# A diffusion-transformer block on one core: weight combinations and weight norms made side by side in a room each, packed rotary tables, and attention's output weights split one stage earlier

## The chip, the core and the metric

The kernel runs on one core of a Trainium2 chip. The metric is device time in microseconds (us) from the program's start to its end. A core has five engines that take their instructions in order: TensorE (PE, matrix products; its weight loads are listed as PEld), VectorE (DVE), ScalarE (ACT), GpSimd (POOL) and SyncE (SP, which here only issues transfers, DMAs). Each engine waits on semaphores for what others produce, so an instruction that waits holds up everything behind it on its engine. The order of each engine's instructions is fixed when the program is built: a scheduler lays them out by a simulated timeline, and the kernel adds its own edges to it ("issue this after that").

## The reference, cut to what matters

One block over 2048 latent tokens of width 1024, with 256 context tokens (one batch, depth 1, float32):

```python
sh1, sc1, g1, sh2, sc2, g2 = split(silu(c) @ w_ada + b_ada)        # the same for the context's c_ctx
hx = rms_norm(x, norm1_g) * (1 + sc1) + sh1
fx, qx, kx, vx = split_projection(hx @ w_in)                        # 512 Fourier columns, 8 heads of 64
qx, kx = axial_rope(rms_norm(qx, q_norm_g)), axial_rope(rms_norm(kx, k_norm_g))
y_four = fourier_mix(fx)                                            # 2-D FFT, real part
y_attn = neighbourhood_attention(qx, kx, vx, kc, vc, rpb)           # 8 x 16 windows and all context keys
g_f, g_a = split(sigmoid(hx @ w_branch_gate))
mixed = (g_f * (y_four @ w_fourier_out) + g_a * (y_attn @ w_attn_out)) @ w_out
x = x + g1 * mixed
hx2 = rms_norm(x, norm2_g) * (1 + sc2) + sh2
x = x + g2 * (relu(hx2 @ w_mlp1) ** 2 @ w_mlp2)
```

## The kernel before

Every large product is made of float16 matmuls: each operand is split into a high and a low half by a scale that is a power of two, and three products of halves replace one product in float32. A scale needs a norm of its weights (a sum of squares over the whole matrix, or its largest row), so weights are read once for a norm and once for the split. The two MLP products use a scheme with 7 block products in place of 8, so their weights are read, combined by additions on DVE, split on ACT (high) and DVE (low), and written to DRAM as combinations ("blocks", `w1d` and `w2d`) that the MLP streams later.

**The projection stage** runs through eight pairs of 256-column units (`seq`): the Fourier columns; gates 4 and 5; query half 0 with gate 0; query half 1 with gate 1; values; key half 0 with gate 2; key half 1 with gate 3; gates 6 and 7. `run_pair(n)` runs pair n; the order of the matmuls is that of the program, and beside them side work is laid out by counting. After each tile of a unit comes `tick(share)`: a gate or Fourier tile counts 2, a 256-column tile of q, k or v counts 1. A tick advances two things. `pace[0]` steps per two ticks are taken of the generators in `beside` (first `side_work`). Once `side_work` has ended, the tick's share times a rate from `RATE[n]` is added to a counter, and each whole unit of it takes one step of `early_blocks`. A "step" is what a generator does up to its next `yield`. Everything in a tick is ordered behind the last eviction of a projection tile on ACT.

**What the side work is.** `side_work` sums the adaLN columns (`ada_load` fetches 1 MB, `ada_sum` makes two DVE sums of 128 x 1024), with the products of the rope tables and the q and k gains in between (`rope_products`), then takes the squares of the first four pieces of both MLP weights (`mlp_norms(range(4))`, a fetch of 1 MB into tile `w12m` and an ACT Square of 128 x 2048 each) and makes their scales (`mlp_scales(0)`). `early_blocks` then prepares six jobs of MLP blocks (`prepare`: each fetches 1 MB into `raw`, and makes 7 combinations; the fetch for the next job is issued in step 1 of the present one), the gate rows g1 and g2 (`gate_rows`), the squares of the other 24 pieces (`mlp_norms(range(4, 16))`) and their scales. All of these fetch into the two buffers of one tag, `awt`. `mlp_norms` holds two pieces: the Square of a piece comes after the fetch of the next but one. What is left of `early_blocks` when the last pair begins is issued there at once.

**The last pair** (gates 6 and 7) has `fourier_prep` beside it at a pace of four steps per tick: squares of the output weights (`norm`, one room `fn`), the folding of the Fourier columns, their channel transform (`channel_dft`, matmuls into `pc`), the split of the Fourier output weights, and small sums. Its last small step takes the norms of `w_attn_out` and `w_out` (`pwn`, a product with ones that sums over partitions) and makes `mgs[:, 0:1]`, the scale with which `w_attn_out` is split.

**Attention** then runs 64 places (4 pairs of heads x 4 row blocks x 4 column blocks) of two blocks each. `block` computes scores, bias and row maximum (one DVE instruction), the exponential (ACT), transposes (PE), the high half (ACT) and the low half (DVE) of the probabilities, and the product with the values. `step` interleaves the stages of consecutive blocks and takes `n_fill` steps of a filler, `beside_attention`: the merge of the Fourier branch (`merge_fourier`, 208 matmuls), then `load_wa`, which fetches `w_attn_out` on POOL's queue and splits it into tile `wa` in eight steps (one ACT and one DVE instruction of 128 x 512 each), and from place 54 on the first tile of the attention output (`attn_out(0)`). A second generator, `gating` (`output_weights`), fetches `w_out` and multiplies it by the gate row and splits it on POOL; `merge_fourier` takes two or three steps of it behind the stores of each of its eight parts. The filler gets one step per block, and from place 8 on a second one at every fourth block. At the last column block of a row block the attention output is transposed, scaled on ACT into `yo` and stored to `yA` from ACT's queue.

**The rope tables** (`load_rope`) hold the cosine and the sine twice, for q and for k: each of the four copies is fetched from a 2048 x 64 table into 128 partitions, so in pieces of 64 floats.

After attention come the output products (`po`) with the rest of the attention outputs, and the MLP with its block products (`pm`, `p`) in two halves of the tokens, beside which the other MLP blocks are prepared.

## Time and profile before

| | |
|---|---|
| median of 3 runs | 2572.53 us (2568.15 to 2574.7) |
| the profiled execution | 2573.11 us, span 2571.3 us |
| granted TensorE clock in it | 0.997 of full speed |
| busy | PE 2492.5 us, DVE 1774.4 us, ACT 1208.9 us, POOL 447.6 us |
| transfers | 509.50 MB, 198 GB/s on average |

The profiled execution's own time is 1.8 us more than its span. The profile gives, for each engine, when it was busy and, for an idle stretch, what ended it. A view by windows cuts the span into stretches and gives the busy time of each engine in them with the granted clock of TensorE (1.00 is full speed) and the busy share of the DMA engines; "x" numbers are counts of instructions. A view of one tile lists the instructions that write or read it, with the shortest, median and longest duration in ns. In a timeline a row ends in square brackets with the idle time before the instruction and what ended it. Matmuls are pipelined: one of 512 columns is listed with about 379 ns while the next starts after 216 ns, so busy time of PE is not a count of work, but idle time is time in which nothing ran. Line 85 (L85) is the matmul of a helper for all split products, and L1053 and L1054 are the two instructions of the helper `pair_of`; such groups are told apart by their tiles.

### The profile page before, as it was taken

The numbers are of one execution on the slowest core, as the hardware profiler recorded it, in microseconds if no ns is written. First come the engines' busy times: TensorE is split into PE (matmuls) and PEld (weight loads), VectorE is DVE, ScalarE is ACT, GpSimd is POOL, SyncE is SP. The second block draws the span as 40 slices with busy tenths as digits, with TensorE's granted clock in tenths as the row PEclk, the third lists the DMA queues.
The fourth block names the chain that finished last, engine by engine and source line by source line (L and its number), as shares of the span: only waits on it lengthen the run. The fifth ranks groups of instructions, "written<-read, shape, count | busy, mean of one in ns | idle before, by whom it ended". The sixth has DMA issues, their size and how long they took to land.

```text
span 2571.3 us, 41720 instructions
## 1 busy us (share of the span) xinstructions
PE 2492.5 (97%) x15706; PEld 1426.5 (55%) x15706; DVE 1774.4 (69%) x3592; ACT 1208.9 (47%) x2131; POOL 447.6 (17%) x567
## 2 busy tenths in 40 slices
PE   7999999999899999999999999999999999999999
PEld 4546668866554677786664444444444444444444
DVE  7755676574453888987885878979777635546367
ACT  7714544325553788964444646445450524223150
POOL 1101220021121567610000121211212000000000
PEclk9999999999999999999999999999999999999999
DMA  8784726547874576656778777777876433333334
GB/s 298 225 271 152 239 82 212 185 151 237 278 262 136 174 214 185 193 177 225 254 242 292 248 263 252 249 246 243 270 266 217 119 95 111 99 103 94 111 103 156
DMA packets 224866, 509.50 MB, mean 198 GB/s; under 512 B 33868, under 2 KB 87884, under 8 KB 209304
## 3 DMA queue, kind: packets, MB, share of 16 engines
q1 hardware_dynamic: 190632, 384.05, 46.6%
q0 software_dynamic: 27264, 91.59, 10.2%
q10 hardware_dynamic: 6768, 31.20, 3.6%
q8 instruction: 123, 2.02, 0.3%
q14 instruction: 79, 0.65, 0.1%
HBM read 367.26 MB, written 137.39 MB: 196 GB/s over the span
## 4 chain that ended last, share of the span: by engine, by line
PE 68%; DMA 11%; DVE 10%; ACT 5%; issue 4%; POOL 1%; SPq 0%; ACTq 0%; DVEq 0%; POOLq 0%
PE p L85 20%; PE pm L85 19%; PE po L85 5%; PE ps_g L85 4%; PE pua L85 2%; PE ps_f L85 2%; PE tp L1638 2%; PE ps_q L85 2%; PE ps_v L85 2%; DMA w12m<-in_w_mlp 2%; PE pv L1652 2%; PE pmf L1573 1%; DMA w12m<-in_w_mlp1t 1%; PE sc L1616 1%; DMA w1d<-wo 1%
## 5 line engine op out<-in xcount | busy, mean ns | idle before, releaser
L85 PE MATMUL pm<-hc,wb 128*128 128x512 f16 x2688 | 582.6, 379 | 5.6 <-DVE u L1935 3.5
L85 PE MATMUL p<-wb,a 128*128 128x512 f16 x2688 | 581.9, 379 | 2.3 <-DVE X L2060 1.7
L85 PEld LDWEIGHTS <-wb 128*128 128x128 f16 x2688 | 263.0, 98 | 323.5 <-issue 7.2
L85 PEld LDWEIGHTS <-a 128*128 128x128 f16 x2688 | 263.0, 98 | 320.0 <-issue 3.2
L2060 DVE SCALAR_TENSOR_TENSOR X<-p,msc,X 128x512 f32<-128x512 f32 x280 | 201.3, 745 | 157.3 <-PE p L85 139.0
L85 PEld LDWEIGHTS <-w_g 128*128 128x128 f16 x1536 | 150.3, 99 | 167.0 <-issue 0.9
L85 PE MATMUL ps_g<-hx,w_g 128*128 128x512 f16 x768 | 171.4, 379 | 0.0
L85 PE MATMUL ps_g<-hx_room,w_g 128*128 128x512 f16 x768 | 171.3, 379 | 0.0
L85 PE MATMUL po<-wo,mH 128*128 128x512 f16 x512 | 152.6, 379 | 1.3 <-DVE ga L1699 1.3
L1935 DVE TENSOR_TENSOR u<-pm,u 128x512 f32<-128x512 f32 x128 | 87.3, 688 | 84.4 <-PE pm L85 82.9
L414 ACT ACTIVATE wo<-ws,msc 128x512 f16<-128x512 f32 x96 | 69.0, 718 | 148.5 <-DVE ws L456 113.9
L1939 ACT ACTIVATE p<-pm 128x512 f32<-128x512 f32 x32 | 18.9, 590 | 239.3 <-PE pm L85 239.3
L1625 DVE CUSTOM_DVE_ANT_0 s<-sc,bt,qsc 128x736 f32<-128x736 f32 (+5 forms) x128 | 110.9, 866 | 21.3 <-PE sc L1619 15.0
L85 PEld LDWEIGHTS <-hx_room 128*128 128x128 f16 x1152 | 113.8, 99 | 19.0 <-DVE qn_k L608 1.6
L85 PEld LDWEIGHTS <-hx 128*128 128x128 f16 x1152 | 113.4, 99 | 18.0 <-DVE qn_k L608 1.9
L1646 DVE SCALAR_TENSOR_TENSOR pL<-tp,pH 128x640 f16<-128x640 f32 (+1 forms) x128 | 112.3, 877 | 11.1 <-ACT pH L1641 10.3
L2071 POOL DMA_DIRECT2D xr<-x1d x32 | 17.3, 540 | 569.3 <-DVE X L1935 563.1
L1629 ACT ACTIVATE s<-s,m 128x736 f32<-128x736 f32 (+5 forms) x128 | 104.7, 818 | 13.1 <-DVE m L1625 13.0
L414 ACT ACTIVATE wo<-raw,msc 128x512 f16<-128x512 f32 x128 | 87.9, 710 | 42.1 <-DVE raw L456 15.1
L1638 PE MATMUL tp<-ident,s 128*128 128x128 f32 x704 | 102.6, 280 | 4.5 <-ACT s L1629 4.3
L543 ACT ACTIVATE ot_g<-ps_g,usc_g 128x512 f32<-128x512 f32 x64 | 43.4, 681 | 132.7 <-PE ps_g L85 74.6
L415 DVE SCALAR_TENSOR_TENSOR wo<-raw,msc,wo 128x512 f16<-128x512 f32 x128 | 94.2, 744 | 15.1 <-ACT wo L414 15.0
(573 smaller groups left out, 4485.3 us busy)
## 6 DMA issues: line engine op xcount, KB each, us to landing
wb<-w1d SPq DMA_DIRECT2D x224, 256.0 KB
wb<-w2d SPq DMA_DIRECT2D x224, 256.0 KB
raw<-in_w_mlp ACTq DMA_DIRECT2D x24, 1024.0 KB
w2d<-wo POOLq DMA_DIRECT2D x86, 256.0 KB, 3.9
w1d<-wo POOLq DMA_DIRECT2D x84, 256.0 KB, 3.8
gT<-ot_g SPq DMA_DIRECT2D x64, 256.0 KB
w12m<-in_w_mlp1t SPq DMA_DIRECT2D x16, 1024.0 KB
w12m<-in_w_mlp SPq DMA_DIRECT2D x16, 1024.0 KB
```

What stands on the lines that cost most here:

```text
L85: last_mm[0] = pe.matmul(ps, l, r, start=(start and i == 0), stop=(stop and i == n - 1))
L414: act.activation(hi, src, AF.Copy, scale=scale)
L415: dve.scalar_tensor_tensor(out=lo, in0=src, scalar=scale, in1=hi, op0=ALU.mult, op1=ALU.subtract)
L543: last_out[0] = act.activation(o, ps, func, scale=scale, bias=bias)
L1573: pe.matmul(ps, l, r, start=(i == 0), stop=(i == len(prods) - 1))
L1625: tail["dve"] = dve.tensor_tensor_reduce(out=s[:, :n], in0=sc, in1=bias, op0=ALU.add, op1=ALU.min, scale=qsc[:, 4:5], scalar=3.0e38, accum ...
L1629: tail["act"] = act.activation(s[:, :n], s[:, :n], AF.Exp, bias=m1[:, 0:1], scale=-1.0, accum_out=m1[:, 1:2])
L1638: tail["pe"] = pe.transpose(tp[:, i * 128:(i + 1) * 128], s[:, o:o + 128], ident)
L1646: tail["dve"] = dve.scalar_tensor_tensor(out=pL[:, :c], in0=tp[:, :c], scalar=PTOP, in1=pH[:, :c], op0=ALU.mult, op1=ALU.subtract)
L1652: tail["pe"] = pe.matmul(pv, p_[:nk, i * 128:(i + 1) * 128], vv[:nk, h2 * 128 + o:h2 * 128 + o + 64], start=(j == 0 and i == 0), stop=(j = ...
L1935: last["dve"] = dve.tensor_tensor(out=o, in0=x, in1=y, op=op)
L2060: last["dve"] = dve.scalar_tensor_tensor(out=X[x], in0=ps, scalar=down if op == ALU.subtract else up, in1=X[x], op0=ALU.mult, op1=ALU.add)
```

## The change

- `ada_load`, `mlp_norms` and others take their room from `big_room`: two tags of one buffer, `awt0` and `awt1`, used in turn unless a number is given.
- `gate_rows` moves from behind the early MLP blocks to `side_work`, ahead of the first squares. The pace is 3 in pair 1 and 2 in pairs 2 to 6 (before: 3, 3, then 2).
- `early_blocks` keeps only the six jobs of blocks, all in room `awt0`; the fetch of the next job is issued in step 6, and each job ends in two empty steps. The other 24 squares become a generator of their own, `other_norms`, in room `awt1`: fetch, step, Square, step. Both run side by side with a rate each, in pairs 3 to 6.
- The rope tables are laid out on the host as 128 x 1024, fetched once each (into the half for q), and the products for k come before those for q.
- `w_attn_out` gets its norm, scale and split in `fourier_prep` (`attn_norm`, `attn_scale`, and twice `attn_load` and `attn_split`), with the halves stored to a DRAM scratch `waD`. In attention four fetches from `waD` on SP's queue replace `load_wa`; the filler's second step comes at every sixteenth block.
- `merge_fourier` takes `gating` steps after each half of a part, behind the copy that opens the part, one per half (two from part 4 on), and `output_weights` issues one fetch per step.
- `yA` is stored from SP's queue, and the low half of the first attention output tile (`yaL`) is made on DVE, not POOL.

The diff, cut to its core:

```diff
+    waD = scratch("waD", [4, 128, 2048], F16)
...
+    def big_room(name, i=None):
+        if i is None:
+            i = turn_of[0] = 1 - turn_of[0]
+        return pb.tile([128, KT, 256], F32, tag=f"awt{i}", name=name).rearrange("p k n -> p (k n)")
...
+        yield from gate_rows()
         yield from mlp_norms(range(N_OWN))
         yield from mlp_scales(0)
...
-                           2, sp.dma_start, sp.dma_start)
+                           2, sp.dma_start, sp.dma_start, False)
         del jobs[:N_EARLY]
-        yield from gate_rows()
-        yield from mlp_norms(range(N_OWN, 16))
+
+    def other_norms():
+
+        for kind in range(2):
+            for j in range(N_OWN, 16):
+                wt = big_room(f"w12m{kind}_{j}", 1)
+                sp.dma_start(wt, a[("w_mlp1t", "w_mlp2")[kind]][j])
+                yield
+                with tc.issue_after(last_out[0].ins):
+                    act.activation(wt, wt, AF.Square, accum_out=(w1m, w2m)[kind][:, j:j + 1])
+                yield
         yield from mlp_scales(1)
...
-                if j == 1:
+                if j == (1 if ahead else 6):
                     fetch(n + 1)
+                yield
+            if not ahead:
+                yield
                 yield
...
-    blocks = [early_blocks(), 0.0, False]
+    blocks, begun = [[early_blocks(), 0.0, 0.0], [other_norms(), 0.0, 0.0]], [False]
...
+            if begun[0]:
+                for o in blocks:
+                    o[1] += share * o[2]
+                    while o[1] >= 1.0:
+                        o[1] -= 1.0
+                        next(o[0], None)
...
             both = pb.tile([128, 2, 16, 64], F32, tag="r" + nm, name=f"r{nm}")
+            sp.dma_start(both[:, 0].rearrange("p t d -> p (t d)"), a[nm])
...
-    RATE = (0, 0, 0.2, 0.25, 0.5, 1.0, 0.9, 0)
+    RATE = ((0, 0),) * 3 + ((0.2, 0.3), (0.4, 0.45), (0.6, 0.55), (0.6, 0.55), (0, 0))
...
-        pace[0] = 8 if n == len(seq) - 1 else (0, 3, 3, 2)[min(n, 3)]
+        pace[0] = 8 if n == len(seq) - 1 else (0, 3, 2)[min(n, 2)]
...
+        def attn_norm():
+            dve.tensor_reduce(out=mgs[:, 12:13], in_=wn[:, 0:2], axis=AX.X, op=ALU.add)
+            spread(mgs[:, 7:8], mgs[:, 12:13], "pwa")
+            pool.tensor_tensor(mgs[:, 7:8], mgs[:, 7:8], half[:, 0:1], op=ALU.pow)
...
+        def attn_split(i):
+            for k in range(2):
+                o = (both[:, k] if i == 0 else (both[:, 1], mix[:, 1])[k]).bitcast(F16).rearrange("p (n o t) -> p n o t", n=2, o=2)
+                for n in range(2):
+                    pair_of(o[:, n, 0], o[:, n, 1], x_room[:, k, n * 512:(n + 1) * 512], mgs[:, 0:1])
+                    yield
+                sp.dma_start(waD[2 * i + k], o.rearrange("p n o t -> p (n o t)"))
...
+                with tc.issue_after(stored.ins):
+                    for _ in range(1 + (m >= 4)):
+                        next(gating, None)
             for h in range(2):
-                i = pool.dma_start(mF[m, :, h * 1024:(h + 1) * 1024], o[h])
-            with tc.issue_after(i.ins):
-                for _ in range(2 if m < 2 else 3):
-                    next(gating, None)
+                pool.dma_start(mF[m, :, h * 1024:(h + 1) * 1024], o[h])
...
-            act.dma_start(yA[hp, :, rb * 512:(rb + 1) * 512], yo)
+            sp.dma_start(yA[hp, :, rb * 512:(rb + 1) * 512], yo)
...
-        eng = dve if t else pool
+        eng = dve
...
-        yield from load_wa()
+        for k in range(4):
+            sp.dma_start(wa[:, k].rearrange("p n o t -> p (n o t)"), waD[k])
+        yield
...
-            step(block(hp, rb, cb, h2, yp), 1 + (n >= 8 and (2 * n + h2) % 4 == 0))
+            step(block(hp, rb, cb, h2, yp), 1 + (n >= 8 and (2 * n + h2) % 16 == 0))
```

More of the change, by code (lines that the diff above doesn't have):

```diff
@@ L341, in mlp_norms @@
             if kind < 2:
-                wt = pb.tile([128, KT, 256], F32, tag="awt", name=f"w12m{kind}_{j}", bufs=2).rearrange("p k n -> p (k n)")
+                wt = big_room(f"w12m{kind}_{j}")
                 sp.dma_start(wt, a[("w_mlp1t", "w_mlp2")[kind]][j])
@@ L477, in dit_block @@
     beside, pace = [side], [0]
-    ticks, rate = [0], [0.0]
-    blocks = [early_blocks(), 0.0, False]
+    ticks = [0]
+    blocks, begun = [[early_blocks(), 0.0, 0.0], [other_norms(), 0.0, 0.0]], [False]
     def tick(share):
@@ L490, in tick @@
                     if next(o, o) is o and o is side:
-                        blocks[2] = True
-            if blocks[2]:
-                blocks[1] += share * rate[0]
-                while blocks[1] >= 1.0:
-                    blocks[1] -= 1.0
-                    next(blocks[0], None)
+                        begun[0] = True
+            if begun[0]:
[4 more added lines that the diff above has]
+                        next(o[0], None)
     def load_raw(w, c0, name):
@@ L578, in load_rope @@
             both = pb.tile([128, 2, 16, 64], F32, tag="r" + nm, name=f"r{nm}")
+            sp.dma_start(both[:, 0].rearrange("p t d -> p (t d)"), a[nm])
             for i, qk in enumerate("qk"):
-                r = both[:, i]
-                sp.dma_start(r, a[nm].rearrange("(t p) d -> p t d", p=128))
-                rope[nm, qk] = r
+                rope[nm, qk] = both[:, i]
     def rope_products(i):
-        r, g = rope[("cos", "sin")[i // 2], "qk"[i % 2]], gain["qk"[i % 2]]
-        dve.tensor_tensor(out=r, in0=r, in1=g.unsqueeze(1).broadcast_to([128, 16, 64]), op=ALU.mult)
+        nm, qk = ("cos", "sin")[i // 2], "kq"[i % 2]
+        dve.tensor_tensor(out=rope[nm, qk], in0=rope[nm, "q"], in1=gain[qk].unsqueeze(1).broadcast_to([128, 16, 64]), op=ALU.mult)
     turned = []
@@ L710, in dit_block @@
     wide = [t.bitcast(F32).rearrange("p o k t -> p (o k t)") for t in hx_rooms]
-    x1_rooms = [pb.tile([128, KT, 256], F32, tag="awt", name=f"x1_{i}", bufs=2).rearrange("p k n -> p (k n)") for i in range(2)]
+    x1_rooms = [big_room(f"x1_{i}") for i in range(2)]
     ada_rooms = [wide[i][:, o:o + 2048] for i in (1, 0) for o in (0, 2048)]
@@ L894, in first_tokens @@
     def first_tokens():
-        r = [pb.tile([128, KT, 256], F32, tag="awt", name=f"h0{o}", bufs=2).bitcast(F16).rearrange("p k n -> p (k n)") for o in "HL"]
+        r = [big_room(f"h0{o}").bitcast(F16) for o in "HL"]
         r = [t.rearrange("p (k t) -> p k t", t=512) for t in r]
@@ L986, in run_pair @@
             return first_pair()
-        rate[0] = RATE[n]
-        pace[0] = 8 if n == len(seq) - 1 else (0, 3, 3, 2)[min(n, 3)]
+        for o, r in zip(blocks, RATE[n]):
+            o[2] = r
+        pace[0] = 8 if n == len(seq) - 1 else (0, 3, 2)[min(n, 2)]
         wu, new = pair(n), [load_pair_unit(n + 1, u) for u in range(2)] if n + 1 < len(seq) else []
@@ L1183, in fourier_prep @@
         yield
+        attn_norm()
         x_scale(1)
@@ L1187, in fourier_prep @@
         rows_split(1, 0)
+        attn_scale()
         yield
@@ L1214, in fourier_prep @@
         yield
+        yield from attn_split(0)
+        attn_load(1)
         x_square(3)
@@ L1223, in fourier_prep @@
         x_scale(3)
+        yield from attn_split(1)
         yield from channel_dft(3)
@@ L1267, in fourier_prep @@
         dve.tensor_reduce(out=mgs[:, 4:5], in_=g1r, axis=AX.X, op=ALU.max, apply_absolute_value=True)
-        for i, (j, n) in enumerate(((0, 2), (2, 4))):
-            dve.tensor_reduce(out=mgs[:, 12 + i:13 + i], in_=wn[:, j:j + n], axis=AX.X, op=ALU.add)
-        spread(mgs[:, 7:9], mgs[:, 12:14], "pwn")
-        pool.tensor_tensor(mgs[:, 7:9], mgs[:, 7:9], half[:, 0:2], op=ALU.pow)
+        dve.tensor_reduce(out=mgs[:, 13:14], in_=wn[:, 2:6], axis=AX.X, op=ALU.add)
+        spread(mgs[:, 8:9], mgs[:, 13:14], "pwn")
+        pool.tensor_tensor(mgs[:, 8:9], mgs[:, 8:9], half[:, 0:1], op=ALU.pow)
         yield
-        dve.tensor_copy(mgs[:, 6:7], mgs[:, 7:8])
-        power_of_two(mgs[:, 6:7], HTOP, 1.0e-9)
-        dve.reciprocal(mgs[:, 0:1], mgs[:, 6:7])
         o = mgs[:, 8:9]
@@ L1296, in dit_block @@
         if n == len(seq) - 1:
-            for o in beside + blocks[:1]:
+            for o in beside + [o[0] for o in blocks]:
                 for _ in o:
@@ L1703, in attn_out @@
             yield
-    def load_wa():
-        raws = [py.tile([128, D], F32, tag=f"y{k // 2}{'HL'[k % 2]}", name=f"wao{k}") for k in range(4)]
-        for k in range(4):
-            pool.dma_start(raws[k], a["w_attn_out"][0, k * 128:(k + 1) * 128, :])
-        for _ in range(6):
-            yield
-        for k in range(4):
-            for n_ in range(2):
-                pair_of(wa[:, k, n_, 0], wa[:, k, n_, 1], raws[k][:, n_ * 512:(n_ + 1) * 512], mgs[:, 0:1])
-                yield
     def beside_attention():
```

22 lines of the change are left out of this document (15 added, 7 removed).

## The prediction

> **What bounds the kernel now.** I read the page first, then the span cut into stretches along the projection pairs, then who waits for whom on PE and ACT, then the timeline at the longest PE wait, the chain of waits, and single tiles. The page's totals, then the stretches (pair 1 is 120 to 203, pairs 2 and 3 reach to 404, values to 500, the two key pairs to 600 and 706, last gates to 814, attention 840 to 1143, MLP from 1430):
>
> ```profile
> span 2571.3 us, 41720 instructions
> PE 2492.5 (97%) x15706; PEld 1426.5 (55%) x15706; DVE 1774.4 (69%) x3592; ACT 1208.9 (47%) x2131; POOL 447.6 (17%) x567
> ...
> core 0: us, PE busy (x) PEld busy (x) DVE busy (x) ACT busy (x) POOL busy (x), PEclk, DMA share, GB/s
> ...
> 120.00:203.00 83.00, 80.35 (x379) 36.86 (x377) 52.19 (x130) 22.83 (x28) 1.19 (x2) 1.00 0.73 239
> 203.00:288.00 85.00, 81.62 (x548) 54.30 (x547) 40.44 (x135) 38.25 (x69) 14.44 (x17) 0.98 0.61 209
> 288.00:404.00 116.00, 112.64 (x791) 77.78 (x789) 88.95 (x275) 57.65 (x121) 26.69 (x25) 1.00 0.44 150
> 404.00:500.00 96.00, 94.37 (x865) 84.27 (x864) 54.51 (x128) 36.17 (x67) 1.12 (x2) 1.00 0.50 166
> 500.00:600.00 100.00, 97.46 (x697) 68.33 (x695) 70.21 (x201) 33.19 (x63) 21.24 (x21) 1.00 0.50 161
> 600.00:706.00 106.00, 96.09 (x639) 64.28 (x638) 46.74 (x148) 63.65 (x93) 19.13 (x18) 0.97 0.85 289
> 706.00:814.00 108.00, 99.79 (x542) 53.86 (x541) 50.66 (x151) 48.60 (x76) 16.62 (x20) 1.00 0.54 190
> ...
> 840.00:1040.00 200.00, 193.15 (x2403) 151.43 (x2401) 172.71 (x399) 162.22 (x361) 128.27 (x126) 0.99 0.63 183
> 1040.00:1100.00 60.00, 53.87 (x754) 46.20 (x753) 56.25 (x124) 55.59 (x127) 37.47 (x35) 1.00 0.76 214
> 1100.00:1143.00 43.00, 41.30 (x565) 36.57 (x563) 39.10 (x90) 33.57 (x78) 8.18 (x8) 1.00 0.44 138
> ...
> 1430.00:2571.30 1141.30, 1130.04 (x5232) 511.62 (x5229) 789.15 (x1207) 430.03 (x687) 116.67 (x215) 1.00 0.55 178
> ```
>
> PE is the bound: 2492.5 of 2571.3 us. The change adds one tiny PE product and removes none, so it can gain only where PE idles: the stretch's length less PE's busy time. That is 9.9 us at 600 to 706, and there the clock column takes 3% of 106 = 3.2 us more: 13.1 us, the worst stretch. 203 to 404 has 3.4 + 3.4 idle and 2% of 85 = 1.7 in the clock: 8.5. 404 to 500 has 1.6, 500 to 600 has 2.5, the last gates 8.2, attention 6.9 + 6.1 + 1.7. The MLP's 11.3 are out of the change's reach.
>
> What makes the 13.1 us:
>
> ```profile
> ACT w12m L340 <- DMA w12m<-in_w_mlp: 19.3, 11, 3.1
> ACT w12m L340 <- DMA w12m<-in_w_mlp1t: 13.5, 8, 3.2
> ```
> ```profile
> L340 ACT ACTIVATE w12m<-w12m x32: 1901/1911/1916, 252.4 to 695.7; 128x2048 f32<-128x2048 f32 x32
> L340 ACT ACTIVATION_READ_ACCUMULATOR w12m<-w12m x32: 183/187/204, 254.2 to 697.5; 128x1 f32 x32
> ```
> ```profile
> 646.76 1.91 ACT L340 ACTIVATE w12m<-w12m 128x2048 f32<-128x2048 f32 x1 [3.05 <-DMA w12m<-in_w_mlp]
> 648.58 0.19 ACT L340 ACTIVATION_READ_ACCUMULATOR w12m<-w12m 128x1 f32 x1
> ...
> 648.93 0.37 ACT L644 ACTIVATE sH_k<-tq_k 128x256 f16<-128x256 f32 x1
> ...
> 649.40 0.41 DVE L645 TENSOR_TENSOR sL_k<-tq_k,sH_k 128x256 f16<-128x256 f32 x1
> ...
> 649.87 0.48 PE L634 MATMUL tq_k<-ident,qr_k 128*128 128x128 f32 x1 [4.36 <-DVE sL_k L645]
> ```
> ```profile
> 624.23 4.93 DMA w12m<-in_w_mlp1t
> ...
> 689.73 10.09 DMA fn<-in_w_fourier_out
> ```
>
> Twenty or so Squares come back to back. Each holds ACT for its wait on the fetch (32.8 us over 19 of them, 1.7 each) and then 1.91 + 0.19 us; behind it stand the key's evictions (sH_k), behind those DVE (sL_k), behind that PE, 4.36 us here. The chain of waits over this stretch is fetch, Square, fetch, Square; a fetch of 1 MB lands after 4.93 us at best there, and the slowest, a first one for the last gates, takes 10.09.
>
> **Norms and combinations side by side.** The same 24 fetches and Squares, and six jobs of combinations, are spread over pairs 4 to 6. Counting from the code: values give 36 shares, a key pair 34, so `other_norms` gets 16.2 + 18.7 + 18.7 of its 54 steps and one in pair 3; the combinations get 14.4 + 20.4 + 20.4 of their 56. Both end with the last key pair, and about one step is left to issue there. A share lasts 96 / 36 = 2.7 us in the values and 206 / 68 = 3.0 in the key pairs, so a Square comes every two steps, 11 to 12 us apart, where its single room needs 4.9 to 10.1 us for the fetch and 2.1 for the Square, 7 to 12 us. It fits, mostly. A Square that finds its fetch one step (5.5 us) old may hold ACT for 0 to 4.6 us, but then ACT has 6 us before the next, where now it has 2. Only six Squares are left in the last key pair. I expect it to idle like its sister pair now, 2.5 us with the same matmuls: 13.1 - 2.5 = **10 us gained**. The bounds are 13 (all of it) and -10 (the first rival below). Values and first key pair get eight or nine Squares each, and the first key pair loses the gate rows; I leave their 1.6 + 2.5 as they are. Combinations keep their instructions; their single raw room is refilled over three steps, 16 us, which covers 10.09.
>
> **Gate rows, pace.** They move from 500 to 535 into pairs 2 and 3:
>
> ```profile
> L281 DVE CUSTOM_DVE_ANT_0 awtg<-awtg,silb x16: 1215/1220/1226, 499.5 to 533.2; 128x1024 f32<-128x1024 f32 x16
> ```
> ```profile
> PE tq_k L634 <- DVE sL_k L645: 6.1, 2, 4.4
> PE pms L359 <- DVE msd L354: 3.6, 2, 3.4
> PE pu_g L520 <- DVE usc_g L521: 2.8, 1, 2.8
> ```
>
> 16 sums of 1.22 us are 19.5 us of DVE, and their 8 fetches queue on SP. DVE is idle 45 us in 203 to 288 and 27 in 288 to 404, and combinations leave pair 3. The `pms` wait (3.4 us, and the clock's 1.7 us right behind it) came of three steps between the last Square and PE's product at 1.5 steps a tick; at one a tick the product has half as much time again. Against that, gate rows, Squares and scales fill 203 to 404 to the last tick but two. I take 3 of its 8.5 us as gained (0 to 6).
>
> **Last gates.** They get 8 more steps of 51 (64 are offered): 8 halves on ACT and on DVE, two 1 MB fetches and four stores on SP in front of the norm fetches and the gate stores, and a sum over partitions (`pwa`) one step behind a Square:
>
> ```profile
> L1053 ACT ACTIVATE wa<-wao,mgs x8: 736/760/775, 1056.2 to 1068.2; 128x512 f16<-128x512 f32 x8
> L1054 DVE SCALAR_TENSOR_TENSOR wa<-wao,mgs,wa x8: 725/736/2496, 1057.8 to 1070.1; 128x512 f16<-128x512 f32 x8
> ```
> ```profile
> 812.93 0.16 DVE L1079 COPY mgs<-pwn 128x2 f32<-128x2 f32 x1 [16.30 <-PE pwn L1078]
> ```
>
> That is 6 us on each of two engines that are idle half of these 108 us. PE idles 8.2 us for 51 steps, so 1.3 us for 8 more, and 0.7 for `pwa`: **2 us lost**. If all eight pairs and both fetches stood on the path it would be 8 x (0.76 + 0.74) + 5 = 17. The cover is DVE's 16.3 us of idleness before the last step; gone, the last small sums slip into the sequence transform behind it, which doesn't read them.
>
> **Attention.** The eight splits leave 1056 to 1073, where DVE is the bound (56.25 of 60 us) and PE idles 6.1. DVE loses 7 x 0.74 + 2.5 = 7.6 us, and the merge, at 17/16 steps a block for 5/4, reaches from place 43 to 49, so that this idle stretch has matmuls. I take the whole 6.1. Added is the low half on DVE, at the stretch where it is busy 39.10 of 43:
>
> ```profile
> L1682 DVE TENSOR_TENSOR yaL<-yat,yaH x7: 1206/1215/1226, 1125.5 to 1321.3; 128x1024 f16<-128x1024 f32 x7
> L1682 POOL TENSOR_TENSOR yaL<-yat,yaH x1: 2137/2137/2137, 1095.4 to 1095.4; 128x1024 f16<-128x1024 f32 x1
> ```
> ```profile
> L1666 ACTq DMA_DIRECT2D yA<-yo x16: 326/326/350, 869.7 to 1144.6; - x16
> ```
>
> 1.2 us on DVE, so **5 us gained** (-4 to 9). The 16 stores free 5.2 us of ACT, which isn't the bound: nothing. On SP they stand among prefetches whose buffers come free no earlier than the row block that the store ends. The `wa` fetches wait on SP for the last merge matmul at place 49; queued behind them is the next q. Eight blocks later, about 15 us, PE needs them: 2 MB behind one another, about 10 us at twice 4.93. If they came late, PE would lose up to 4. `gating` keeps its work, and each piece moves ahead of the `mF` stores on POOL, which is idle 72 of 200 us: nothing, down to 2 us lost where a bias table queues behind it.
>
> **Rope tables.** Two fetches for four, of 4 KB pieces for 256-byte ones.
>
> ```profile
> L581 SPq DMA_DIRECT2D rcos<-in_cos x2: 647/3567/6487, 72.4 to 73.1; - x2
> L586 DVE TENSOR_TENSOR rcos<-rcos,gaink x1: 1218/1218/1218, 131.5 to 131.5; 128x1024 f32<-128x1024 f32 x1
> ```
>
> They are issued near 72 and first read at 131, and PE idles 2.7 us in all of 120 to 203: nothing. The Trainium skill ("DMA: Bandwidth & Descriptors", Specifications) asks for transfers of at least 512 bytes for line rate; by it the queue would empty sooner; no row here shows the two sizes apart, and it moves no term of this sum.
>
> **Sum.** -10 - 3 + 2 - 5 = -16 us from 2573.1 (the profiled execution, 0.6 above the median): **2557 us**. Bounds of the terms together reach 2545 to 2565.
>
> **The rivals.**
> (1) The single room holds ACT, slower. If a fetch lands later than about 9 us, the room's cycle passes 11 us and every Square meets an unlanded fetch, now through all of 404 to 706. At the present price, 13.1 us per 106, that is 302 / 106 x 13.1 = 37 us in place of 17.2: +20, and +14 with the other terms: 2587. For: one fetch of 10.09, and combinations now fetch and store beside. Against: the rows near 5 us were taken at a DMA share of 0.85, which spreading lowers. The Trainium skill ("Trainium Kernel Development and Optimization", Best Practices) asks for two buffers so that transfers overlap compute; by that rule this is the likely case, but the trace's waits are from two rooms. Chance 0.09.
> (2) The waits move with the Squares: 24 of them cost 13.1 wherever they stand. Then -3 + 2 - 5: 2567. Chance 0.13.
> (3) The last gates run over by the 17 us above: 2572. Chance 0.07.
> (4) A generator falls behind, its Squares come at once where the last gates begin, at 4 us each for three: 2569. The count speaks against it. Chance 0.04.
> The forecast keeps 0.67. A measurement here tells about 0.3%, 7.7 us, from no change. Faster by more (below 2565): the forecast, and some of (2): 0.70. Slower by more: (1), and a bad end of (3): 0.11. The rest 0.19. The range leaves out (1) and the far tail below: 2543 to 2573.
>
> **What would show it.** Right: PE idle near 3 us and clock 1.00 in the last key pair; Squares about 11 us apart with waits below 4; no `wa` splits after 1040 and PE idle under 2 there; the last gates' idle near 10. Wrong: more than 60 us of ACT waiting on `w12m`, a PE wait over 3 us on tq_k with the clock below 1.00 behind it, or PE waiting on `wa` or on `pc` for a split.

## The result: 22 us faster, more than forecast, and partly in other places

The changed kernel takes 2548.5 us (median of 5 runs, 2540.68 to 2548.97), the kernel before beside it 2570.19 us (5 runs, 2568.15 to 2574.7). The ratio is 0.9904, 95% interval 0.989 to 0.9919. The profiled execution is the one of 2548.5 us; its span is 24.6 us shorter than that of before (2571.3 - 2546.7). The forecast was 16 us.

The page's totals of the changed kernel first:

```profile
span 2546.7 us, 41747 instructions
PE 2490.3 (98%) x15708; PEld 1428.7 (56%) x15708; DVE 1774.9 (70%) x3594; ACT 1210.8 (48%) x2131; POOL 444.0 (17%) x563
```

PE's busy time, in which slowed matmuls count too, is 2.2 us less than before (2492.5), so 22.4 of the 24.6 us are idle time of PE. Where they went is read from the first and last starts of the same tiles. The view of single tiles, kernel before (the last two times in a row are the group's first and last start):

```profile
L85 PE MATMUL ps_q<-w_q,hx x384: 269/273/417, 212.9 to 392.7; 128*128 128x256 f16 x192
...
L85 PE MATMUL ps_v<-w_v,hx x384: 269/273/273, 398.2 to 495.5; 128*128 128x256 f16 x192
...
L85 PE MATMUL ps_k<-w_k,hx x384: 269/273/283, 495.6 to 693.3; 128*128 128x256 f16 x192
...
L1619 PE MATMUL sc<-k,Q x256: 271/272/417, 840.1 to 1136.2; 128*128 128x256 f16 x128
...
L85 PE MATMUL po<-wo,mH x512: 376/379/379, 1151.6 to 1393.5; 128*128 128x512 f16 x171
```

The same rows of the changed kernel:

```profile
L85 PE MATMUL ps_q<-w_q,hx x384: 269/273/421, 211.7 to 393.5; 128*128 128x256 f16 x192
...
L85 PE MATMUL ps_v<-w_v,hx x384: 269/273/273, 399.0 to 494.1; 128*128 128x256 f16 x192
...
L85 PE MATMUL ps_k<-w_k,hx x384: 269/273/283, 494.2 to 674.2; 128*128 128x256 f16 x192
...
L1663 PE MATMUL sc<-k,Q x256: 271/272/421, 814.9 to 1112.9; 128*128 128x256 f16 x128
...
L85 PE MATMUL po<-wo,mH x512: 379/379/379, 1128.3 to 1368.7; 128*128 128x512 f16 x171
```

| stretch, between two of these starts | before, us | changed, us | difference | forecast |
|---|---|---|---|---|
| up to the first ps_q | 212.9 | 211.7 | -1.2 | 0 |
| first ps_q to first ps_v (pairs 2 and 3) | 185.3 | 187.3 | +2.0 | -3 |
| first ps_v to first ps_k (values) | 97.4 | 95.2 | -2.2 | 0 |
| first to last ps_k (key pairs) | 197.7 | 180.0 | -17.7 | -10 |
| last ps_k to first sc (last gates, sequence transform) | 146.8 | 140.7 | -6.1 | +2 |
| first sc to first po (attention) | 311.5 | 313.4 | +1.9 | -5 |
| first po to the end of the span | 1419.7 | 1418.4 | -1.3 | 0 |

One profile is one execution. In the changed kernel and five runs below whose code is the same up to there, the first ps_q stands between 209.7 and 211.7, the first ps_v between 396.6 and 402.0, and the key pairs take 180.0 us in all six. From the last ps_k to the first sc, the changed kernel and four runs with the same code in that stretch take 139.9 to 143.0 us. The -17.7 and the -6.1 are outside that, the others near it, and are read by the waits inside them. "sc" is the first product of attention; the rows taken are those of its 256-column group. The windows of the changed kernel, with the columns as in the prediction:

```profile
286.00:399.00 113.00, 110.16 (x748) 75.54 (x747) 70.33 (x235) 60.79 (x118) 25.89 (x25) 0.97 0.51 171
399.00:494.00 95.00, 95.00 (x873) 85.26 (x872) 51.58 (x124) 48.50 (x79) 1.71 (x2) 1.00 0.67 222
494.00:588.00 94.00, 94.00 (x677) 66.37 (x676) 63.56 (x182) 49.42 (x82) 20.62 (x20) 1.00 0.71 243
588.00:686.00 98.00, 98.00 (x686) 67.39 (x685) 61.02 (x181) 42.09 (x75) 21.97 (x22) 1.00 0.54 178
...
1013.00:1073.00 60.00, 55.48 (x764) 46.35 (x762) 52.22 (x121) 49.64 (x117) 38.86 (x39) 0.99 0.75 222
1073.00:1118.00 45.00, 42.16 (x554) 37.04 (x554) 39.41 (x87) 35.66 (x80) 8.00 (x8) 0.94 0.45 130
```

From 399 to 686, PE has no idle time at all and the full clock: the values and both key pairs now run at PE's own pace, though they carry all 24 Squares and nearly all the combinations. What the Squares cost ACT is in its waits (in all, times, longest; window 399 to 690) and in the tile's row:

```profile
ACT w12m L423 <- DMA w12m<-in_w_mlp: 10.9, 4, 4.7
...
ACT w12m L423 <- DMA w12m<-in_w_mlp1t: 2.5, 2, 1.6
```
```profile
L423 ACT ACTIVATE w12m<-w12m x24: 1895/1906/1918, 405.2 to 647.1; 128x2048 f32<-128x2048 f32 x24
```

ACT waits 13.4 us on six fetches, where it waited 32.8 us on nineteen. One wait is 4.7 us long, longer than the 3.1 that stopped PE before, and PE does not notice: it seems that ACT can catch up before the next Square. The 24 start between 405.2 and 647.1, 10.5 us apart on average (241.9 / 23). Single ones stand closer: those at 603.84, 611.65 and 619.75 are 8 us apart, with waits of 4.7, 2.7 and 0 us, and PE runs on.

Two stretches did not gain, and in each a new wait has taken the place of an old one. At 373 us, in the timeline, and in the window behind it:

```profile
371.55 0.69 DVE L473 TENSOR_TENSOR ws<-raw 128x512 f32<-128x512 f32 x1 [2.58 <-DMA raw<-in_w_mlp]
...
376.03 0.56 PE L541 MATMUL pu_v<-usc_v,ones 128*128 128x1 f32 x2 [2.85 <-DVE usc_v L542]
```
```profile
376.00:382.00 6.00, 5.97 (x29) 4.50 (x30) 4.50 (x18) 2.90 (x5) 0.91 (x1) 0.50 0.09 19
```

DVE waits for the first raw piece of the combinations; behind it in DVE's order stand the small sums of the value units' scales, and PE waits 2.85 us for those. Then its clock is at half for 6 us. In attention, the chain of waits and the timeline:

```profile
1059.67 8.35 DMA yA<-yo
1068.15 4.73 DMA yat<-yA
```
```profile
1074.09 0.37 PE L85 MATMUL pua<-yaH,wa 128*128 128x256 f16 x1 [4.67 <-ACT yaH L1725]
```

The same store in the chain of the kernel before:

```profile
1088.41 2.08 DMA yA<-yo
```

This store, the last that the first output tile needs, takes 8.35 us to land (2.08 us before), then it is fetched back, and PE waits 4.67 us; the clock column has 0.94 in the 45 us behind that, 2.7 us more.

### The profile page after: what moved, and what is told of

The parts are those of the page before. It is cut to its first block, busy times and chain, and to the rows that moved or that the text cites. A ratio compares the mean times of both kernels' runs of the same rounds, so it can differ in the third digit from the quotient of the medians.

```text
span 2546.7 us, 41747 instructions
## 1 busy us (share of the span) xinstructions
PE 2490.3 (98%) x15708; PEld 1428.7 (56%) x15708; DVE 1774.9 (70%) x3594; ACT 1210.8 (48%) x2131; POOL 444.0 (17%) x563
## 4 chain that ended last, share of the span: by engine, by line
PE 50%; DVE 5%; ACT 2%; issue 2%; DMA 1%; POOL 0%; DVEq 0%; ACTq 0%; SPq 0%; POOLq 0%
PE p L85 20%; PE pm L85 18%; PE po L85 6%; PE pua L85 3%; DVE X L1969 1%; DVE a L1969 1%; DVE u L1969 1%; DVE wo L432 1%; ACT a L1973 1%; PE tp L1682 1%; ACT u L1973 1%; DVE X L2094 0%; PE pv L1696 0%; PE tpb L1860 0%; ACT wo L431 0%
## 5 line engine op out<-in xcount | busy, mean ns | idle before, releaser
L1669 DVE CUSTOM_DVE_ANT_0 s<-sc,bt,qsc 128x736 f32<-128x736 f32 (+5 forms) x128 | 110.9, 867 | 26.9 <-PE sc L1663 20.3
L85 PEld LDWEIGHTS <-hx_room 128*128 128x128 f16 x1152 | 112.6, 98 | 16.1 <-DVE qn_q L628 0.3
```

Of the source, the lines that this page charges most:

```text
L85: last_mm[0] = pe.matmul(ps, l, r, start=(start and i == 0), stop=(stop and i == n - 1))
L1669: tail["dve"] = dve.tensor_tensor_reduce(out=s[:, :n], in0=sc, in1=bias, op0=ALU.add, op1=ALU.min, scale=qsc[:, 4:5], scalar=3.0e38, accum ...
```

## The experiments

The theory after this reading: PE lost time where Squares stood so close that ACT had no time to catch up, and spreading them is the gain; attention lost what it won because transfers on the path now share their time with prefetches. The rival: it is the order of the parts (gate rows out of the key pairs, emptier queues) that counts, not the distance of the Squares. Ratios are to the kernel before on the same chip; the intervals are 95%.

**The distance of the Squares.** The changed kernel with the Squares kept for the key pairs:

```diff
-    RATE = ((0, 0),) * 3 + ((0.2, 0.3), (0.4, 0.45), (0.6, 0.55), (0.6, 0.55), (0, 0))
+    RATE = ((0, 0),) * 3 + ((0.2, 0), (0.4, 0), (0.6, 0.8), (0.6, 0.8), (0, 0))
```

> The changed kernel with other rates: the 24 norm squares wait for the two key pairs (rates 0, 0, 0.8, 0.8 in place of 0.3, 0.45, 0.55, 0.55), so one comes every 7.5 us in place of every 11; one room as in the changed kernel. Theory: the room's cycle of 7 to 12 us no longer fits, ACT waits some 1 to 4 us on most fetches with the key's evictions behind it, and the two key pairs together lose 6 to 14 us of PE with the clock below 1.00 in one of them: 2554 to 2563 us. Rival (the density does not matter; the gain comes from the order of the parts, with the gate rows gone from the key pairs): 2547 to 2550 us.

Measured: 2581.45 us, ratio 1.0035 (1.0023 to 1.0048): slower than the kernel before, and 33 us slower than the changed one. The row of the Squares, ACT's waits (window 399 to 720), then the windows of the two key pairs:

```profile
L423 ACT ACTIVATE w12m<-w12m x24: 1900/1911/1925, 505.2 to 690.5; 128x2048 f32<-128x2048 f32 x24
```
```profile
ACT w12m L423 <- DMA w12m<-in_w_mlp: 46.0, 12, 5.5
...
ACT w12m L423 <- DMA w12m<-in_w_mlp1t: 39.1, 10, 5.4
```
```profile
492.00:599.00 107.00, 97.34 (x669) 67.41 (x668) 62.09 (x176) 51.48 (x85) 18.74 (x18) 0.95 0.65 218
599.00:716.00 117.00, 105.02 (x703) 69.96 (x702) 61.04 (x176) 53.40 (x88) 22.29 (x24) 0.97 0.63 203
```

The rates ask for a Square every 7.5 us; in the trace they come 8.1 us apart (185.3 / 23). 22 of 24 Squares find no data and hold ACT for 85.1 us, 3.9 each; PE idles 9.7 and 12.0 us and loses 5% and 3% of its clock, and its largest group of waits in 492 to 716 is for the key's evictions on DVE, which stand behind ACT's (`sL_k`, 11.3 us in four waits). This is the mechanism of the forecast's first rival, on the real kernel: with one room the fetch can only start when the Square has ended, so the room's cycle is fetch plus Square. The Square of 621.80 shows it: with its small read it takes 1.91 + 0.19 us, the next fetch is issued at 623.83, and the next Square starts at 630.27. Asked for every 7.5 us that does not fit, at 10.5 us on average it does. The gate rows are out of the key pairs in this run too, so the order of the parts alone does not make the gain. The loss was larger than expected (33 us, not 6 to 14): in the profiles the key pairs take 206.4 us for 180.0, and the last gates behind them 150.9 for 140.7. The Trainium skill ("Trainium Kernel Development and Optimization", Best Practices) asks for double buffers to overlap transfers with compute. At 10.5 us the changed kernel shows one buffer to be enough; that two would have been enough at 7.5 us no run here shows.

**The same with two rooms, by rates alone.** The kernel before, with the combinations hurried over the values so that the Squares can start sooner:

```diff
-    RATE = (0, 0, 0.2, 0.25, 0.5, 1.0, 0.9, 0)
+    RATE = (0, 0, 0.2, 0.25, 1.0, 0.7, 0.67, 0)
```

> The kernel before with other rates alone (0.2, 0.25, 1.0, 0.7, 0.67 in place of 0.2, 0.25, 0.5, 1.0, 0.9): the combinations run faster over the values, so that the squares start earlier and come every 4.4 us in place of every 3.3, from the same two rooms, still one after the other with the combinations. Theory (the density of squares makes the stall, whoever shares the time): the last key pair loses half of what it loses in the kernel before, 5 to 9 us fewer: 2562 to 2567 us. Rival (combinations at a step a share stall the values in turn, or two rooms at 4.4 us still wait for every fetch): 2570 to 2577 us.

Measured: 2571.11 us, ratio 1.0 (0.9985 to 1.0014): nothing, as the rival had it. Its profiled execution is the fastest of its twelve runs (2565.69 us), so only its distribution is read. The rows of the Squares from 495 us on, before and in this run, then the windows of the values and the last key pair:

```profile
L340 ACT ACTIVATE w12m<-w12m x24: 1902/1911/1916, 596.0 to 695.7; 128x2048 f32<-128x2048 f32 x24
```
```profile
L340 ACT ACTIVATE w12m<-w12m x24: 1902/1911/1918, 566.9 to 669.5; 128x2048 f32<-128x2048 f32 x24
```
```profile
398.00:498.00 100.00, 95.69 (x870) 84.77 (x868) 65.61 (x153) 39.07 (x73) 2.13 (x3) 1.00 0.64 215
...
594.00:690.00 96.00, 89.94 (x641) 63.70 (x639) 45.77 (x145) 58.48 (x88) 18.14 (x19) 0.98 0.78 259
```

The Squares start and end sooner, but stand 4.5 us apart (102.6 / 23) where they stood 4.3 us apart (99.7 / 23): these rates moved them and hardly spread them, so this run does not test the distance. The last key pair still idles 6.1 us, and the values, which idled 1.6 us before, idle 4.3 with the hurried combinations beside them. In the changed kernel both kinds of work have the whole 275 us from 399 to 674. That no better set of rates exists for the old order is not shown.

**The parts by themselves.** First the kernel before with all of the change but attention's part:

```diff
+        yield from gate_rows()
...
+    blocks, begun = [[early_blocks(), 0.0, 0.0], [other_norms(), 0.0, 0.0]], [False]
...
+    RATE = ((0, 0),) * 3 + ((0.2, 0.3), (0.4, 0.45), (0.6, 0.55), (0.6, 0.55), (0, 0))
```

> The kernel before with the projections' part and the rope tables alone (norms and combinations side by side, gate rows in the side work, new rates); splits of the attention weights, yA stores, yaL and the gating pieces stay as before. Theory: all of the gain is made before attention and attention gives some 5 of it back, so the first psq-to-attention point comes 24 to 29 us sooner and the end is at 2543 to 2548 us, no later than the changed kernel's 2548.5. Rival, the forecast's own sum (attention gains 5, its splits cost 2 in the last gates): 3 us later than the changed kernel, 2551 to 2553.

Then the kernel before with attention's part alone:

```diff
+        yield from attn_split(0)
...
+            sp.dma_start(yA[hp, :, rb * 512:(rb + 1) * 512], yo)
...
+            sp.dma_start(wa[:, k].rearrange("p n o t -> p (n o t)"), waD[k])
```

> The kernel before with attention's part alone: splits beside the last gates, wa fetched from DRAM, yA stores on SP, yaL on DVE, gating in smaller pieces; norms, gate rows and rope tables as before. Theory: the late yA store costs attention some 8 us where the splits had cost 6, and the last gates, whose DMA queue is still full of norm fetches here, pay 2 to 8 for the splits: 2573 to 2581 us. Rival, the forecast's sum of these two terms (+2 and -5): 2567 us. If the splits stand on the path, as the forecast's third rival had it, 2585 or more.

Measured: 2551.34 us, ratio 0.9915 (0.99 to 0.993), for the first, 2569.66 us, ratio 0.999 (0.9981 to 0.9999), for the second. The projections make nearly all of the gain. Attention's part by itself is worth 0.1%, about 2.6 us, with an interval that all but reaches no change, and on top of the projections' part it is not told from nothing (0.9915 and 0.9904, with overlapping intervals). So the part does not lose as the theory had it. The 3 us that the forecast had for it lie inside the interval, but its profile does not show them: there the kernel is 4.1 us ahead at the last ps_k, where its code is still that of before, and 3.2 us ahead at the end. Projections alone:

```profile
L85 PE MATMUL ps_k<-w_k,hx x384: 269/273/283, 491.9 to 671.9; 128*128 128x256 f16 x192
...
L1639 PE MATMUL sc<-k,Q x256: 271/273/417, 814.9 to 1110.3; 128*128 128x256 f16 x128
...
L85 PE MATMUL po<-wo,mH x512: 376/379/379, 1125.6 to 1366.8; 128*128 128x512 f16 x171
```

Attention's part alone:

```profile
L85 PE MATMUL ps_k<-w_k,hx x384: 269/273/421, 492.7 to 689.2; 128*128 128x256 f16 x192
...
L1643 PE MATMUL sc<-k,Q x256: 271/272/421, 834.8 to 1132.9; 128*128 128x256 f16 x128
...
L85 PE MATMUL po<-wo,mH x512: 376/379/379, 1148.3 to 1389.3; 128*128 128x512 f16 x171
```

From the last ps_k to the first sc it is 146.8 us before, 145.6 with attention's part alone, 143.0 with the projections alone, 140.7 with both. So the eight splits show no cost in the last gates; that the stretch is 1 to 2 us shorter with them is inside the spread of single executions. And attention takes 311.5 us before, 310.7 with the projections alone, 313.5 with its own part alone and 313.4 in the changed kernel, but 311.2 with the same part in the next run: neither the forecast's 5 us nor a sure loss.

**Rope tables.** The changed kernel with the four fetches of 256-byte pieces put back:

```diff
-            sp.dma_start(both[:, 0].rearrange("p t d -> p (t d)"), a[nm])
+                r = both[:, i]
+                sp.dma_start(r, a[nm].rearrange("(t p) d -> p t d", p=128))
```

> The changed kernel with the rope tables as before: four fetches of 256-byte pieces in place of two of 4 KB pieces. The forecast's term: nothing, 2547 to 2550 us, the rope products on DVE at the same place near 133 us and no PE wait for them. Rival, by the rule that pieces under 512 bytes lose line rate: the queue empties later at 72 to 130 us and the next unit's weights behind the tables come late; PE's first stretches lose 1 to 4 us: 2550 to 2553 us.

Measured: 2548.51 us, ratio 0.9911 (0.9894 to 0.9929), against 0.9904 with the packed tables. The packing moves no time that these runs can tell.

**The late store in attention.** Four runs on it. The first puts the store on ACT's queue:

```diff
-            sp.dma_start(yA[hp, :, rb * 512:(rb + 1) * 512], yo)
+            act.dma_start(yA[hp, :, rb * 512:(rb + 1) * 512], yo)
```

> The changed kernel with one edit: attention's yA stores go out on ACT's queue again, not on SP's. Theory: the store at 1059.67 us took 8.35 us to land because it stood behind the four 1 MB-and-more wa fetches on SP's queue; with it gone from there, PE's 4.67 us wait for yaH and the half clock behind it (6.8 us, 3.4 lost) go, so the kernel ends 7 to 8 us sooner than the changed one: 2540 to 2542 us. Rival: the pair's yat fetch or the wa fetches are late whatever queue the store is on; then PE waits for one of them instead and the time stays at 2547 to 2550.

Measured: 2547.19 us, ratio 0.99 (0.9884 to 0.9916): no gain, and the store, now on its own queue, is as late. The chain of waits:

```profile
1062.33 7.88 DMA yA<-yo
```

So the queue is not the cause. This theory fell; the next was that the 2 MB of `wa`, fetched just ahead of the store, fill the DMA engines. Three empty steps for the filler between the fetch of `yat` and its first use:

```diff
+        if t == 0:
+            for _ in range(3):
+                yield
```

> The changed kernel with edit (b) alone: three empty filler steps of about 1.6 us between the first yat fetch and its first use. Theory, after the run with the store on ACT's queue (it still took 7.88 us to land there and PE still waited 4.1 us): the store and the fetch are slow because the 2 MB of wa are in flight at the same time, on whatever queue; giving them three more steps takes PE's 4.8 us and the 3.4 us of half clock behind them: 2540 to 2543 us. Rival: the late start leaves steps of the filler over at attention's end, or PE then waits for wa: 2546 to 2550 us.

Measured: 2548.65 us, ratio 0.9907 (0.9884 to 0.9929). PE's wait fell from 4.7 to 2.2 us in the profile, and the time did not. The wait differs between executions: 2.9 to 4.9 us in five kernels without the empty steps (the changed one and four runs), 2.2 to 3.3 us in four with them. Nor is all of it due to `wa`: with the projections alone, where these fetches are not made, the store lands in 2.10 us and PE still waits 2.2 us there. Then `wa` in two halves of 1 MB, the second written behind the first product:

```diff
+            if t == 0 and m == 1:
+                load_wa(1)
```

> The changed kernel with wa fetched in two halves of 1 MB and nothing else. Theory (2 MB of wa in flight make yA's store land after 8.35 us): the store lands after 4 to 5 us and PE's wait of 4.7 us for yaH falls to 1 or 2, 3 to 5 us under the changed kernel with its clock: 2543 to 2546 us. Rival (wo's fetches or the traffic of this stretch at large make the store late): the store still takes 7 us or more, 2547 to 2550 us.

Measured: 2547.57 us, ratio 0.9907 (0.989 to 0.9924). This run tells nothing of its question, as the timeline of SP shows:

```profile
1052.55 8.74 SPq L1753 DMA_DIRECT2D wa<-waD  x8
1061.47 0.32 SPq L1710 DMA_DIRECT2D yA<-yo  x1
```

The scheduler pulled the second half ahead of the store again, so the same 2 MB stood in front of it. The last run holds the order by edges: `wa` behind the store, and the first combinations behind the split of the value weights on DVE (cut to these two; in it are also the three empty steps above, edit (a) of the next part, and rates of 0 and 0.43 for the combinations in pairs 3 and 4):

```diff
+            with tc.issue_after(yA_out[0].ins):
+                for k in range(4):
+                    sp.dma_start(wa[:, k].rearrange("p n o t -> p (n o t)"), waD[k])
...
+                with tc.issue_after(low[0].ins) if not ahead and n == 0 else nullcontext():
```

> The changed kernel with the edits (a) and (b) of the run of three, and two orders held by edges of their own, since in the runs before the scheduler had put both back: the first combinations on DVE come behind the split of the value weights (rates 0 and 0.43), and the four wa fetches are issued behind yA's store, not ahead of it. Theory: (1) the first raw sums stood on DVE ahead of the value units' small scales, so the pu_v wait at 373 (2.9 to 4.7 us in all runs so far) and the 3.4 us of half clock behind it go; (2) yA's store had shared the DMA engines with 2 MB of wa, so it lands after 2 to 3 us in place of 8. Together 6 to 9 us under the run of three: 2534 to 2538 us. Rival to (1): the pu_v wait stays over 2.5 us. Rival to (2): the store still takes 7 us, or it lands early and PE then waits as long for wa itself; with both rivals 2542 to 2546 us.

Measured: 2545.43 us, ratio 0.9893 (0.9865 to 0.9922). Both mechanisms are there, and neither is seen in the time. The chain in attention, PE's wait, and the windows around the first combinations:

```profile
1052.87 2.37 DMA yA<-yo
1055.38 10.74 DMA yat<-yA
```
```profile
PE pua L85 <- ACT yaH L1733: 2.9, 1, 2.9
```
```profile
286.00:399.00 113.00, 113.00 (x803) 79.34 (x801) 71.82 (x243) 62.59 (x122) 25.83 (x25) 1.00 0.52 173
399.00:495.00 96.00, 94.00 (x861) 83.86 (x859) 51.27 (x123) 48.79 (x80) 1.12 (x2) 1.00 0.69 233
```

With `wa` behind it, the store lands in 2.37 us; now it is the next fetch, `yat`, that takes 10.74 us in place of 4.73, and PE waits 2.9 us. Neither theory (2) nor its rival had named this transfer: the bytes in flight are the cause as far as these runs go, and the small transfer that stands beside them is late. The busy share of the DMA engines fits: 0.90 and 0.96 while the store took 8.35 and 7.88 us, 1.02 while `yat` took 10.74, but 0.66 and 0.34 while the store took 2.37 and 2.08. At 286 to 399 PE has no idle time and the full clock, so (1) was the cause of the stop at 373; the values behind it idle 2.0 us again, and the values' first product comes 5.3 us sooner (393.7 for 399.0), the last key product 2.8 us sooner (671.4 for 674.2).

**The stop at attention's start, and the versions put together.** In the changed kernel, POOL's issues and PE's first product with the small rows of the Fourier branch:

```profile
812.36 1.17 POOL L1766 DMA_DIRECT2D wo<-in_w_out  x2
813.52 1.56 POOL L1597 DMA_DIRECT2D s<-y  x3
...
829.58 0.38 PE L1617 MATMUL pmf<-a,w 68*128 68x512 f16 x1 [1.12 <-DVE a L1601]
```

The gating pieces that moved ahead of the `mF` stores moved ahead of this fetch as well. Edit (a) leaves them out of the first part of the merge and takes two per half from the fourth part on:

```diff
-                    for _ in range(1 + (m >= 4)):
+                    for _ in range((0, 1, 1, 2, 2, 2, 2, 2)[m]):
```

> The changed kernel with edit (a) alone: no gating piece (and so no wo fetch) beside the first row of Fourier products. Theory: the wo fetches issued at 812 us, 1 MB, stand in front of s<-y, so that a is ready 3.7 us late and PE waits 1.3 and 1.7 us at 828 to 831, with half clock behind: 3 to 5 us sooner than the changed kernel, 2543 to 2546 us. Rival: the order of the small sums on DVE makes that wait; no change, 2547 to 2550 us.

Measured: 2545.77 us, ratio 0.9893 (0.987 to 0.9916). The rows after it:

```profile
808.00 1.59 POOL L1597 DMA_DIRECT2D s<-y  x3 [0.16 <-POOL mo L1607]
...
822.25 0.38 PE L1617 MATMUL pmf<-a,w 68*128 68x512 f16 x1
```

The fetch is first, and PE no longer waits: 14.3 us from issue to product (822.25 - 808.00) for 16.1 in the changed kernel (829.58 - 813.52). The wait was small: 0.2 to 1.1 us in five executions without (a), none in the four with it. The traces show its cause; the 2.7 us in the medians lie inside the intervals. With (a), (b) the three empty steps, and (c) one empty step ahead of the first combinations (and a rate of 0.43 for 0.4 in the values):

```diff
         fetch(0)
         yield
+        if not ahead:
+            yield
```

> The changed kernel with three edits at three places. (a) The first wo fetches of the gating pieces go two rows of products later, so that they no longer stand in front of the small s<-y fetch at attention's start. (b) Three empty steps of the filler between the first yat fetch and its first use. (c) One empty step between the first raw fetch of the combinations and its first use. Theory: each of the three PE waits (1.3 + 1.7 us at 828, 4.8 at 1069, 3.0 at 373) goes, and with it the half clock behind it (1.7, 3.4 and 3.4 us): about 4, 8 and 6 us, together 14 to 18 us under the changed kernel: 2530 to 2535 us. Rival: the transfers are late because the DMA engines are full, and the waits move to the next user: 2545 to 2549 us.

Measured: 2543.39 us, ratio 0.9889 (0.9865 to 0.9914). With (a), (b), (c), `wa` in halves and the combinations begun in the values by their rates:

```diff
-    RATE = ((0, 0),) * 3 + ((0.2, 0.3), (0.4, 0.45), (0.6, 0.55), (0.6, 0.55), (0, 0))
+    RATE = ((0, 0),) * 3 + ((0, 0.3), (0.45, 0.45), (0.6, 0.55), (0.6, 0.55), (0, 0))
```

> The changed kernel with the edits (a) and (b) of the run of three, wa fetched in two halves of 1 MB (the columns that the first four products use before yA's last store, the others after the first product), and the combinations begun in the values (rates 0 and 0.45 in place of 0.2 and 0.4, one empty step after the first fetch). Theory (small transfers late because large prefetches share the DMA engines, and DVE held in order by the first raw fetch): the pua wait falls from 3.3 us to under 1, the pu_v wait at 373 to under 1 with no half clock behind it; 5 to 10 us under the run of three: 2533 to 2538 us. Rival (the waits belong to the stretch, not to these transfers): 2541 to 2546 us.

Measured: 2542.22 us, ratio 0.9891 (0.9874 to 0.9908). Neither reached what was expected, since the stops at 373 and in attention stayed (PE waits of 3.9 and 3.3 us in the first, 4.1 and 3.1 in the second). In the second the first sum stands where it stood, although its rate is zero there.

```profile
L475 DVE TENSOR_TENSOR ws<-raw x1: 693/693/693, 370.2 to 370.2; 128x512 f32<-128x512 f32 x1
```

An empty step or a rate of zero did not hold it: the sum was written later in the program, and the scheduler still laid it out there. An edge behind the value weights held it (383.4 us in the run with the edges). These two are the fastest versions here. Both are faster than the kernel before; over the changed kernel they have 5 to 6 us in the medians, which the overlapping intervals do not settle.

## Why the prediction was right, and where it was wrong

The sum was -16 and the measurement -22 in the medians, -24.6 in the profiles. The direction and the main mechanism were right: the last key pair was the worst stretch, its loss came from Squares without a pause, and spreading them to 10.5 us removed it. That the total came so near is in part luck: pairs 2 and 3, the last gates and attention were forecast at -6 together and came to -2.2, each with the wrong sign, while the key pairs and values brought 10 us more than their term.

- **Key pairs, -10.** Right in mechanism, too small. The step that was mis-sized is "I expect it to idle like its sister pair now, 2.5 us", together with leaving the "1.6 + 2.5" of values and first key pair as they were. Measured is no idle time in 399 to 686, and -17.7 in the key pairs, -2.2 in the values. The idle time left in a sister stretch was taken as its floor, and it went too; what made it is not separated.
- **Squares 11 us apart, waits under 4.** 10.5 us on average, six waits, the longest 4.7. The last Square starts at 647, not at the end of the pair at 674: the count of steps was a little off. Spread to the end they would have stood further apart still.
- **Pairs 2 and 3, -3.** Wrong: +2.0. The step "I take 3 of its 8.5 us as gained" looked only at the wait that goes. The wait on `pms` did go; in its place came the 2.85 us at 373, where the combinations' first fetch holds DVE ahead of the value units' scales. The run with the edges shows it: without that stop the stretch takes 182.4 us (393.7 - 211.3), 2.9 less than before, which is the forecast's 3. The gate rows' sums on DVE stand beside PE waits of 1.2 and 1.6 us there.
- **Last gates, +2.** Wrong in sign: -6.1, of which some 4 come without the splits (143.0 for 146.8). The step that failed counts steps ("1.3 us for 8 more") as if PE's idle time (8.4 us from the last ps_k to the first sc before, 3.6 now) were spread over them. Part of it came from the first fetches, which had been queued behind the key pair's: the chain before leads from the fetch of `fn` at 689.73 to the last key evictions, and PE waits 1.77 us for one of these at 708.37; the changed kernel has no such wait. The Squares of `fn` begin before and after at:

```profile
L1099 ACT ACTIVATE fn<-fn x8: 1893/1911/1912, 713.6 to 784.2; 128x2048 f32<-128x2048 f32 x8
```
```profile
L1120 ACT ACTIVATE fn<-fn x8: 1900/1910/1913, 691.6 to 759.3; 128x2048 f32<-128x2048 f32 x8
```

  20.3 us behind the last ps_k before (713.6 - 693.3), 17.4 now (691.6 - 674.2). The prediction quoted the fetch of 10.09 us in this place and used it for the room's cycle only. What made the other half of the -6.1 is not separated.
- **Attention, -5.** Wrong: +1.9. "I take the whole 6.1" priced the splits that leave and not what came in their place. The waits that it counts did go: from 1000 to 1140 us PE waits 6.4 us for ACT's `s` and DVE's `pL` before, 0.9 now. Two clauses failed. "On SP they stand among prefetches whose buffers come free no earlier": the `wa` fetches are issued from 1052.18 us, 7.5 us ahead of the store that PE needs, and share the DMA engines with it; PE's wait of 4.7 us and the clock's 2.7 behind it took the gain. And "nothing, down to 2 us lost where a bias table queues behind it", said of `gating`: what queued behind it was `s<-y`, with PE waits of up to 1.1 us. "If they came late, PE would lose up to 4", said of `wa`, was the right transfer with the wrong victim.
- **Rope, 0.** Right.
- **The rivals.** The first one's mechanism is real and shows when a Square is asked for every 7.5 us in place of 10.5; its price came near (2587 forecast for Squares that all wait, 2581.45 measured), though it was worked out for a longer stretch. The second (waits move with the Squares) is refuted by 399 to 686. The third and fourth did not happen.

What stays open is what part of the -17.7 belongs to the gate rows that left the key pairs; no run moved them alone. The profile before gives a bound for their own stall: from 495.6 to 534.5, where their sums stand, PE idles 1.4 us at full clock. What their leaving did by making room for the Squares is not bounded by that.

## What to carry to other kernels

One buffer can be enough for side work when its pieces come further apart than the buffer's usual cycle of fetch and use (about 8 us here: pieces 10.5 us apart stopped nothing, pieces asked for every 7.5 us cost 33 us); so try to spread such work over all the stages that can hold it, two kinds side by side, before giving it a second buffer. When work is taken out of a stage, ask of each transfer left there which larger transfer now starts beside it, and price the small transfers on the path first. Where the program is laid out by a scheduler, hold an order that matters by an edge and read it back from the trace.

## What the hardware showed

- The queue from which a store is issued did not matter when the DMA engines were nearly full: 8.35 us to land on SP's queue behind `wa` (busy share 0.90), 7.88 us on ACT's own (0.96), 2.37 us when it was issued ahead of `wa` (0.66). The Trainium skill ("DMA: Bandwidth & Descriptors", Issuing engines are not separate DMA queues) says so, and these runs agree.
- A wait of PE of 2.85 us was followed by 6 us at half clock (0.50 in 376 to 382), about 3 us lost: the stop cost twice its length. The Trainium skill ("TensorE: Matmul & The Clock Gate", Part 1: The HAM clock gate) puts the idle window that halves the clock at about 3.4 us; here a shorter wait was enough, and the clock fell about 2 us into it (0.69 in 375 to 375.5), while a wait of 2.10 us at 746 left it at 1.00.
